# Softmax weights split into two fp16 parts and transposed by DMA, values into two scaled fp16 parts, in a two-layer attention trunk

## The chip, the core and the metric

The kernel runs on one core of a Trainium2 chip. The core has five engines that run side by side, each working through its own instructions in order: PE (TensorE, matmuls; its weight loads are listed apart as PEld), DVE (VectorE), ACT (ScalarE), POOL (GpSimd) and SP (SyncE, which here issues all DMA transfers). They meet by semaphores. PE reads SBUF and writes PSUM; 16 DMA engines move data between SBUF and the main memory, or within SBUF. The metric is the device time of one execution in microseconds.

## The reference

Two layers over a sequence of 2048 frames with 1024 features, all in float32. Each layer has a norm, one input projection, two groups of attention heads, a gate on each group, and an output projection that is added to the residual.

```python
# layer 0
z = rms_norm(x, ln_g) @ w_in
#   A: 4 heads, each with two score maps over 64 features and values 128 wide
s = q @ k.T * scale - slopes * dist;  p = softmax(masked s)
w = p[:, :, 0] - lam * p[:, :, 1]
a_out = rms_norm(w @ v, subln_g) * (1.0 - lam_init)
#   B: 8 heads, values 64 wide, frame-causal, log forget gates as bias
b_out = softmax(q @ k.T * scale + cq - cum) @ v
x = x + concat([a_out * silu(ag), b_out * silu(bg)]) @ w_out
# layer 1
#   C: 8 query heads on 2 key/value heads, window of two blocks, sinks
#   D: 8 heads, own chunk and 8 chunks before it, learned bias by distance
x = x + concat([c_out * silu(cg), d_out * silu(dg)]) @ w_out
```

All q and k are normed. In A and B a row of scores reaches back to the start of the sequence; in D it covers at most 5 blocks of 128, in C 2.

## The kernel before

The sequence is cut into 16 blocks of 128 rows (tb). The work runs unit by unit: four units of A (one head each), four of B (two heads each), the first output projection, two units of C (four query heads each), four of D (two heads each), the second output projection. Each unit has 16 steps, one per tb.

A step has four parts. `p` projects: 24 matmuls of 128x512 into the tile `z` (lines 213 to 215: input and weight are each split in a high and a low 32-bit part, and three of the four products are kept), then `evac`, `qk_prep`, and the values, split by `v_split` (or inline in A) into V (high and low part side by side, fp32r) and a bf16 copy Vb. `t` transposes q and k. `q` is `qk_row`: logits of up to 512 columns in PSUM (`pss`, line 305), added to a bias and reduced to a minimum by DVE (line 308) into `row`, then one exponential per 1024 columns on ACT (`exp_row`, line 326). `v` multiplies the weights with the values.

PE needs the weights transposed for that. `v` takes four blocks of 128x128 of `row` at a time: PE transposes them into PSUM (`ptp` at line 352, `ptA` at line 470), ACT copies the high part `pth` (fp32r, line 103) and DVE the rest `ptl` (bf16, line 107); then each block is multiplied: `pth` with V (128x128 in B, C and D, line 367; 128x256 in A, line 481), `ptl` with Vb (lines 369 and 484). In A the two score maps are first combined, row = row0 + cf * row1, on DVE (line 467) or, in odd groups of four whole blocks, on POOL (lines 464 and 465).

`drive` sets the order in which the work is written: in round i it merges projection of step i + 2, transposes of q and k of step i + 1, logits of step i, and values of step i - 1, the last from 0.4 of the round on. A scheduler then puts each engine's instructions in order. PSUM has 2 buffers for `z`, 2 for logits (pS), 3 for transposes (pT), 1 for the output of `v` (pO).

Of the kernel before, what the change touches and what calls it, by code (L numbers as in the profile page):

```python
# [25 lines left out]
SCRATCH = 1024  # L26

# [29 lines left out]
class Trunk:  # L57
    def __init__(self, ctx, tc, t):
# [8 lines left out]
        self.sm = pool("sm", 6)  # L67
        self.dram = pool("dram", 1, space=bass.MemoryType.DRAM)
# [14 lines left out]
        for i in range(2):  # L83
            g = self.const.tile([P, KB], F32, name=f"lng{i}")
            nc.sync.dma_start(g[:], t[f"ln{i}"])
            self.lng.append(g)
        self.mhalf = self.const.tile([P, 8], F32, name="mhalf")
# [84 lines left out]
    def transposed(self, xs, dst):  # L172

        nc = self.nc
        for half, x in enumerate(xs):
# [3 lines left out]
            xt = self.ap.tile([P, 4, 2, P], F32R, tag="xn", name="xnT", bufs=2)  # L179
# [15 lines left out]
    def split_x(self, st, src, dst, lo_eng):  # L195
# [3 lines left out]
        for i, (h, l, x) in enumerate(st["x"]):  # L199
            raw = self.wp.tile([P, KB // 2, P], F32, tag="xraw", name="xraw", bufs=2)  # L200
# [58 lines left out]
    def v_split(self, z):  # L259

        nc = self.nc
        V = self.kvp.tile([P, 2, P], F32R, tag="V", name="V", bufs=19)
        V4 = V[:].rearrange("p h (a d) -> p h a d", a=2)
        self.split(V4[:, :, 0], V4[:, :, 1], z.rearrange("p (h d) -> p h d", d=64), nc.scalar, nc.gpsimd)
        Vb = self.kvp.tile([P, 2, 64], BF16, tag="Vb", name="Vb", bufs=19)
        nc.scalar.activation(Vb[:].rearrange("p h d -> p (h d)"), z, AF.Copy)
        return V, Vb

    def silu2(self, z, mul=None):
# [6 lines left out]
        if mul is not None:  # L276
            nc.gpsimd.tensor_tensor(out=g[:], in0=g[:], in1=mul, op=ALU.mult)
# [43 lines left out]
    def exp_row(self, row_st, nmax):  # L321
        nc = self.nc
        s = row_st["sums"]
        rows = row_st["rows"]
        for i, (row, hm) in enumerate(rows):
            nc.scalar.activation(row[:, :hm * P], row[:, :hm * P], AF.Exp, scale=-1.0, bias=nmax, accum_out=s[:, i:i + 1])  # L326

    def two_sums(self, st):

        s = st["s"] = self.sm.tile([P, 2, 2], F32, tag="rs", name="rs")  # L330
        st["r"] = [dict(sums=s[:, h]) for h in range(2)]
# [7 lines left out]
    def heads_av(self, nh, items, r, gate, dst):  # L339
# [3 lines left out]
        groups = [items[i:i + 4] for i in range(0, len(items), 4)]  # L343
        hls = {}
        st = {}

        def tr(gi):
            g = groups[gi]
            n = len(g)
            pt = self.pT.tile([P, 4, P], F32, tag="t", name="ptp")  # L350
            for i, it in enumerate(g):
                nc.tensor.transpose(pt[:, i], it[1](), self.idf[:])  # L352
            h = ap.tile([P, 4, P], F32R, tag="pt", name="pth", bufs=5)
            l = ap.tile([P, 4, P], BF16, tag="ptl", name="ptl", bufs=5)
            hls[gi] = h, l
            self.split(h[:, :n], l[:, :n], pt[:, :n], nc.scalar, nc.vector)

        def mm(gi):
# [3 lines left out]
            h, l = hls[gi]  # L362
            g = list(enumerate(groups[gi]))
            for head in sorted({it[0] for _, it in g}):
                own = [(i, it) for i, it in g if it[0] == head]
                for i, (_, _, V, first, last) in own:
                    nc.tensor.matmul(O[:, head], h[:, i], V[0], start=first, stop=False, skip_group_check=True)  # L367
                for i, (_, _, V, first, last) in own:
                    nc.tensor.matmul(O[:, head, 0:64], l[:, i], V[1], start=False, stop=last, skip_group_check=True)  # L369

        def end():
            O = st["O"]
            o = ap.tile([P, nh, 64], F32, tag="oT", name="oT", bufs=2)
            nc.scalar.activation(o[:], O[:, :, 64:128], AF.Copy, scale=0.5)
            nc.vector.scalar_tensor_tensor(out=o[:], in0=O[:, :, 0:64], scalar=0.5, in1=o[:], op0=ALU.mult, op1=ALU.add)
# [5 lines left out]
        n = len(groups)  # L381
        for gi in range(n + 1):
            if gi < n:
                pieces.append((0.109 * len(groups[gi]), lambda gi=gi: tr(gi)))
            if gi:
                pieces.append((0.095 * len(groups[gi - 1]), lambda gi=gi: mm(gi - 1)))
# [9 lines left out]
    def unit_A(self, h, W, X):  # L396
        nc, ap = self.nc, self.ap
        slope = float(2.0 ** (-8.0 * (h + 1) / 4))
        ks, vs, steps = [], [], []

        def mk(tb):
# [3 lines left out]
            def p():  # L405
# [4 lines left out]
                pieces = self.proj(st, z, W, 512)  # L410
                if h == 0:
                    pieces.append((KB * 0.107, lambda: self.forget(st)))

                def post():
# [6 lines left out]
                    V = self.kvp.tile([P, 2, P], F32R, tag="V", name="VA", bufs=19)  # L421
                    self.split(V[:, 0, :], V[:, 1, :], z[:, 256:384], nc.scalar, nc.gpsimd)
                    Vb = self.kvp.tile([P, P], BF16, tag="Vb", name="Vb", bufs=19)
                    nc.scalar.activation(Vb[:], z[:, 256:384], AF.Copy)
                    vs.append((V, Vb))
# [12 lines left out]
            def q():  # L438
                self.two_sums(st)
                out = []  # L440

                def last():
# [3 lines left out]
                    nc.vector.reciprocal(s[:, :, 1], s[:, :, 0])  # L446
                for c in range(2):
# [3 lines left out]
            def v():  # L451
                hls = {}
                groups = [(j, min(4, m - j)) for j in range(0, m, 4)]

                def tr(gi):
                    r0, r1 = st["r"]
# [619 lines left out]
```

## Time and profile before

| | us |
|---|---|
| runs: median (lowest, highest) | 2948.31 (2943.84, 2950.85) |
| the profiled execution | 2953.78 |
| its span (first to last instruction) | 2951.9 |

The stages in the trace, from the span's start: A to about 805 us, B to 1540, the first output projection to 1800, C to 2160, D to 2760, the second output projection to the end. The projections' 512-column matmuls of layer inputs are the largest groups, over 700 us of busy time each:

```profile
L213 PE MATMUL z<-wh,x 128*128 128x512 f32 x1792 | 729.4, 408 | 16.8 <-DVE x L105 12.9
L352 PE MATMUL ptp<-idf,row 128*128 128x128 f32 x1648 | 256.5, 277 | 0.6 <-DVE ptl L107 0.6
```

A row names the line, engine, operation, the tiles written and read, the shape, the count; then the busy time and the mean of one in ns; then the idle time of the engine just before them and what ended it. Durations of matmuls overlap, so their sum is no time of PE: the distance of two starts is.

### The profile page before, as it was taken

How to read it: one execution, taken by the hardware profiler on the slowest of the kernel's cores; microseconds unless marked ns; L12 is line 12 of the kernel's file. 1: busy time of each engine (PE TensorE's matmuls, PEld its weight loads, DVE VectorE, ACT ScalarE, POOL GpSimd, SP SyncE). 2: the span in 40 equal slices, each digit the busy share in tenths (PEclk: the TensorE clock that was granted, in tenths of full speed). 3: DMA queues.
4: the chain of work that ended last, by engine and by line, in shares of the span. 5: the costliest groups of instructions: out<-in, count | busy, mean ns of one | idle time of the engine just before them, and what ended most of it. 6: DMA issues, size and time to landing. Idle time of an engine off the chain costs nothing.

```text
span 2951.9 us, 53646 instructions
## 1 busy us (share of the span) xinstructions
PE 2876.8 (97%) x18152; PEld 2435.1 (82%) x18152; DVE 1981.1 (67%) x6282; ACT 1834.3 (62%) x4821; POOL 1188.0 (40%) x1852
## 2 busy tenths in 40 slices
PE   7999999999999999999999999999999999999999
PEld 5778778787888888888888887988888888888787
DVE  6898888878877677676775335666666666666422
ACT  6567767677677666676674225777766666666310
POOL 5775565655534324432331003353334343342200
PEclk8999999999999999999999999999999999999999
DMA  8443333332333423333325644244444433342532
GB/s 299 154 133 135 127 117 117 111 125 96 112 102 105 135 86 125 122 99 121 102 67 178 215 186 159 92 135 139 144 141 141 134 132 135 120 159 93 173 129 86
DMA packets 152978, 389.43 MB, mean 132 GB/s; under 512 B 17376, under 2 KB 47072, under 8 KB 152704
## 3 DMA queue, kind: packets, MB, share of 16 engines
q1 hardware_dynamic: 152704, 385.99, 38.6%
q8 instruction: 145, 2.38, 0.3%
q14 instruction: 129, 1.06, 0.1%
HBM read 318.75 MB, written 67.17 MB: 131 GB/s over the span
## 4 chain that ended last, share of the span: by engine, by line
PE 74%; DVE 11%; POOL 5%; ACT 4%; issue 3%; DMA 3%; SPq 0%; POOLq 0%; DVEq 0%; ACTq 0%
PE z L213 11%; PE z L214 11%; PE z L215 11%; PE pss L305 8%; PE ptp L352 7%; PE OT L367 6%; PE zo L213 4%; PE zo L215 4%; PE zo L214 4%; DVE row L308 3%; PE OT L369 2%; PE ptq L247 2%; POOL y L115 1%; DVE ptl L107 1%; DVE row L467 1%
## 5 line engine op out<-in xcount | busy, mean ns | idle before, releaser
L213 PE MATMUL z<-wh,x 128*128 128x512 f32 x1792 | 729.4, 408 | 16.8 <-DVE x L105 12.9
L215 PE MATMUL z<-wh,x 128*128 128x512 f32 x1792 | 717.3, 401 | 4.4 <-POOL x L107 3.6
L214 PE MATMUL z<-wl,x 128*128 128x512 f32 x1792 | 718.2, 401 | 2.7 <-POOL wl L107 1.7
L326 ACT ACTIVATE row<-row,mx 128x1024 f32<-128x1024 f32 (+7 forms) x512 | 440.2, 861 | 186.4 <-DVE mx L308 181.1
L305 PE MATMUL pss<-kT,qT 128*128 128x512 f32 (+3 forms) x1728 | 501.3, 373 | 20.3 <-DVE mx L308 18.5
L213 PEld LDWEIGHTS z<-wh,x 128*128 128x128 f32 x1792 | 342.0, 191 | 76.4 <-ACT wh L152 10.3
L215 PEld LDWEIGHTS z<-wh,x 128*128 128x128 f32 x1792 | 341.2, 190 | 71.1 <-POOL x L107 5.7
L214 PEld LDWEIGHTS z<-wl,x 128*128 128x128 f32 x1792 | 342.0, 191 | 61.5 <-DVE wl L153 4.3
L107 DVE TENSOR_TENSOR ptl<-ptp,pth 128x512 bf16<-128x512 f32 (+1 forms) x518 | 326.2, 640 | 77.1 <-ACT pth L103 74.6
L103 ACT ACTIVATE pth<-ptp 128x512 fp32r<-128x512 f32 (+1 forms) x518 | 276.0, 556 | 123.0 <-PE ptp L352 120.0
L305 PEld LDWEIGHTS pss<-kT,qT 128*128 128x128 f32 x1728 | 292.5, 190 | 62.3 <-DVE mx L308 27.7
L367 PE MATMUL OT<-V,pth 128*128 128x128 f32 x1896 | 314.0, 278 | 0.1
L115 POOL TENSOR_TENSOR y<-v,mhalf 128x4 f32<-128x4 f32 (+2 forms) x326 | 292.2, 898 | 19.4
L367 PEld LDWEIGHTS OT<-V,pth 128*128 128x128 f32 x1896 | 281.9, 193 | 14.6 <-ACT pth L103 0.6
L352 PE MATMUL ptp<-idf,row 128*128 128x128 f32 x1648 | 256.5, 277 | 0.6 <-DVE ptl L107 0.6
L107 POOL TENSOR_TENSOR hl<-zs,hl 128x256 fp32r<-128x256 f32 (+1 forms) x240 | 175.1, 730 | 187.9 <-DVE hl L105 144.2
L221 ACT ACTIVATE zs<-z,rs 128x512 f32<-128x512 f32 (+1 forms) x240 | 160.3, 669 | 118.3 <-PE z L215 110.3
L352 PEld LDWEIGHTS ptp<-idf,row 128*128 128x128 f32 x1648 | 191.2, 142 | 22.5 <-PE pss L305 1.0
L107 POOL TENSOR_TENSOR V<-zs,V 128x128 fp32r<-128x128 f32 x144 | 67.2, 468 | 334.8 <-ACT V L103 331.2
L369 PE MATMUL OT<-Vb,ptl 128*128 128x64 bf16 x1896 | 177.2, 198 | 1.5 <-DVE ptl L107 1.5
L107 POOL TENSOR_TENSOR wl<-wraw,wh 128x512 fp32r<-128x512 f32 x118 | 154.1, 1310 | 46.0 <-ACT wh L103 43.6
L117 DVE TENSOR_TENSOR q<-y 128x4 f32<-128x4 f32 (+2 forms) x326 | 85.6, 263 | 126.5 <-POOL y L115 124.8
(180 smaller groups left out, 5785.8 us busy)
## 6 DMA issues: line engine op xcount, KB each, us to landing
x<-xs SPq DMA_DIRECT2D x416, 512.0 KB, 3.6
wraw<-in_w_dram SPq DMA_DIRECT2D x64, 256.0 KB, 2.8
xs<-x SPq DMA_DIRECT2D x32, 512.0 KB, 4.1
xs<-xnT SPq DMA_DIRECT2D x32, 512.0 KB, 5.2
xraw<-in_xT_dram SPq DMA_DIRECT2D x32, 256.0 KB, 3.9
x<-in_x_dram SPq DMA_DIRECT2D x32, 256.0 KB, 6.0
mixa<-out SPq DMA_DIRECT2D x128, 64.0 KB, 2.0
biasB<-cumd SPq DMA_DIRECT2D x32, 256.0 KB, 4.3
```

The source lines that it names most:

```text
L103: nc.scalar.activation(hi, src, AF.Copy)
L107: lo_eng.tensor_tensor(out=lo, in0=src, in1=h, op=ALU.subtract)
L115: nc.gpsimd.tensor_tensor(out=y[:], in0=v[:], in1=self.mhalf[:, :n], op=ALU.pow)
L213: nc.tensor.matmul(ps(), xh[:, i, :], wh, start=(kb == 0), stop=False)
L214: nc.tensor.matmul(ps(), xh[:, i, :], wl, start=False, stop=False)
L215: nc.tensor.matmul(ps(), xl[:, i, :], wh, start=False, stop=(kb == KB - 1))
L221: self.nc.scalar.activation(zs[:, :n], z[:, :n], AF.Copy, scale=self.rs[layer][:, tb:tb + 1])
L305: nc.tensor.matmul(ps[:, :w], q()[:, j, :], k[:, slot, (b % 4) * P:(b % 4) * P + w], start=(j == 0), stop=(j == 1))
L326: nc.scalar.activation(row[:, :hm * P], row[:, :hm * P], AF.Exp, scale=-1.0, bias=nmax, accum_out=s[:, i:i + 1])
L352: nc.tensor.transpose(pt[:, i], it[1](), self.idf[:])
L367: nc.tensor.matmul(O[:, head], h[:, i], V[0], start=first, stop=False, skip_group_check=True)
L369: nc.tensor.matmul(O[:, head, 0:64], l[:, i], V[1], start=False, stop=last, skip_group_check=True)
```

## The change

The weights are no longer transposed by PE. As soon as a row's exponential is there, `weights_T` splits it where it lies, by rows: ACT writes the high part as fp16, scaled by 2^15 (in A by a factor per row), DVE the low part as fp16 behind it in the same tile `ph`, and one DMA on SP's queue transposes both from SBUF to SBUF into `pT`. `v` then only multiplies, with both operands in fp16. The order of the work in `v` loses the pieces for transposes, and the work of `weights_T` is issued in `q`.

Values become two fp16 parts, V, without Vb. So that they fit fp16, each column of values is scaled by a power of two taken from the sum of squares of its weights' column: `v_scale` computes it once per unit (8 squares on POOL, 8 matmuls with ones, a few integer steps on DVE). DVE multiplies the values by `inv`; the inverse `sc` goes into the gate on POOL (B, C, D) or onto A's output on DVE. In A the coefficients of the combination are worked out in `q`, with four more single-column steps, and every odd group of blocks goes to POOL. The logits get a third PSUM buffer, the transposes lose one; `xraw` and `xnT` share the buffers of `ph` and `pT`.

```diff
-        self.pS = pool("pS", 2, space=bass.MemoryType.PSUM)
-        self.pT = pool("pT", 3, space=bass.MemoryType.PSUM)
+        self.pS = pool("pS", 3, space=bass.MemoryType.PSUM)
+        self.pT = pool("pT", 2, space=bass.MemoryType.PSUM)
...
+    def v_scale(self, W, c, bias):
...
+        def square(kb):
...
+            w = W[kb][0][:, c:c + P].bitcast(F32)
+            nc.gpsimd.tensor_tensor(out=sq[0][:, kb], in0=w, in1=w, op=ALU.mult)
+        def sums():
+            ps = self.pT.tile([P, P], F32, tag="t", name="psw")
+            for kb in range(KB):
+                nc.tensor.matmul(ps[:], self.ones[:], sq[0][:, kb], start=(kb == 0), stop=(kb == KB - 1))
...
+    def v_split(self, z, inv, heads):
+        nc = self.nc
+        nc.vector.tensor_tensor(out=z, in0=z, in1=inv[:], op=ALU.mult)
+        V = self.kvp.tile([P, heads, 2, P // heads], F16, tag="V", name="V", bufs=19)
+        self.split(V[:, :, 0], V[:, :, 1], z.rearrange("p (h d) -> p h d", h=heads), nc.scalar, nc.gpsimd)
+        return V
+
+    def weights_T(self, w, n, scale=PSC):
+        nc, ap = self.nc, self.ap
+        hl = ap.tile([P, 2048], F16, tag="ph", name="ph", bufs=3)
+        nc.scalar.activation(hl[:, :n], w, AF.Copy, scale=scale)
+        nc.vector.scalar_tensor_tensor(out=hl[:, n:2 * n], in0=w, scalar=scale, in1=hl[:, :n], op0=ALU.mult, op1=ALU.subtract)
+        pt = ap.tile([P, 16, P], F16, tag="pt", name="pT", bufs=PTB)
+        nc.sync.dma_start_transpose(out=pt[:, :2 * n // P], in_=hl[:, :2 * n])
+        return pt[:, :2 * n // P].rearrange("p (a b) q -> p a b q", a=2)
...
             nc.scalar.activation(row[:, :hm * P], row[:, :hm * P], AF.Exp, scale=-1.0, bias=nmax, accum_out=s[:, i:i + 1])
+            if row_st.get("T") is not None:
+                row_st["T"].append(self.weights_T(row[:, :hm * P], hm * P))
...
-        def tr(gi):
...
-                nc.tensor.transpose(pt[:, i], it[1](), self.idf[:])
...
-            self.split(h[:, :n], l[:, :n], pt[:, :n], nc.scalar, nc.vector)
...
+            for head, w, V, first, last in own:
+                nc.tensor.matmul(O[:, head], w()[:, 0], V().rearrange("p a d -> p (a d)"), start=first, stop=False, skip_group_check=True)
+            for head, w, V, first, last in own:
+                nc.tensor.matmul(O[:, head, 0:64], w()[:, 1], V()[:, 0], start=False, stop=last, skip_group_check=True)
...
+                    cf = self.sm.tile([P, 4], F32, tag="cf", name="cf")
+                    st["r0"], kap = cf[:, 3:4], cf[:, 2:3]
+                    nc.vector.tensor_scalar(out=cf[:, 0:1], in0=s[:, 1, 1:2], scalar1=s[:, 0, 0:1], scalar2=self.nlam[:, 0:1], op0=ALU.mult, op1=ALU.mult)
+                    nc.vector.scalar_tensor_tensor(out=cf[:, 1:2], in0=cf[:, 0:1], scalar=-1.0, in1=cf[:, 0:1], op0=ALU.mult, op1=ALU.max)
+                    nc.vector.tensor_scalar(out=cf[:, 1:2], in0=cf[:, 1:2], scalar1=1.0 / PSC, scalar2=1.0 / PSC, op0=ALU.mult, op1=ALU.add)
+                    nc.vector.reciprocal(kap, cf[:, 1:2])
+                    nc.vector.tensor_tensor(out=st["r0"], in0=cf[:, 1:2], in1=s[:, 0, 1:2], op=ALU.mult)
...
+                            if i % 2:
+                                nc.gpsimd.tensor_scalar(out=t1, in0=t1, scalar1=cf[:, 0:1], scalar2=1.0, op0=ALU.mult, op1=ALU.mult)
+                                nc.gpsimd.tensor_tensor(out=t0, in0=t1, in1=t0, op=ALU.add)
+                            else:
+                                nc.vector.scalar_tensor_tensor(out=t0, in0=t1, scalar=cf[:, 0:1], in1=t0, op0=ALU.mult, op1=ALU.add)
+                        st["T"].append(self.weights_T(w0[:, :n * P], n * P, kap))
...
+                    nc.vector.tensor_tensor(out=o[:], in0=o[:], in1=u["sc"][:], op=ALU.mult)
```

Three places show what stands in a row. Line numbers of the changed kernel are its own: 218 to 220 are the projection (213 to 215 before), 347 the logits (305), 394 and 396 the high and low product (367 and 369), 485 the combination (467), 198 the load of x (193).

PE in B, block tb = 9 of a unit, before: the weights' transposes stand among the projection's matmuls, and the products close behind them.

```order
L305 MATMUL pss_18872<-kT_18247,qT_18661 128x384 x2
L352 MATMUL ptp_18920<-idf_87,row_18710 128x128 x2
L213 MATMUL z_19048<-wh_15272,x_18641 128x512
L214 MATMUL z_19048<-wl_15273,x_18641 128x512
L215 MATMUL z_19048<-wh_15272,x_18641 128x512
L352 MATMUL ptp_18944<-idf_87,row_18710 128x128 x4
L367 MATMUL OT_18911<-V_16924,pth_18889 128x128
L367 MATMUL OT_18911<-V_17187,pth_18889 128x128
```

The same place now: the products read `pT`, which a DMA wrote; the last logits of that row (`pss_17490`) stand 54 projection matmuls ahead of the first product.

```order
L218 MATMUL z_18135<-wh_13760,x_17756 128x512
L219 MATMUL z_18135<-wl_13761,x_17756 128x512
L220 MATMUL z_18135<-wh_13760,x_17756 128x512
L394 LDWEIGHTS pT_17517
L394 MATMUL OT_17632<-V_15884,pT_17517 128x128
```

No transpose of weights is left on PE, and each product brings its own weight load of a 16-bit block.

SP, the queue of DMAs, in B around the outputs of tb = 8 and 9 (`mixa8`, `mixa9`), before: loads of x, of weights, and the outputs.

```order
L379 DMA mixa8_145<-out_18833 128x128
L193 DMA x_19044<-xs0_15_120 128x1024
L193 DMA x_19256<-xs0_0_105 128x1024
L379 DMA mixa9_146<-out_19040 128x128
L193 DMA x_19257<-xs0_0_105 128x1024
L150 DMA wraw_17963<-in_w0_dram 128x512
```

Now each row of scores adds a transposing DMA per 1024 columns (16 blocks: 8 high, 8 low; 6 blocks: 3 and 3).

```order
L406 DMA mixa8_150<-out_17571 128x128
L307 DMA_TRANSPOSE pT_17621<-ph_17618 128x16x128
L307 DMA_TRANSPOSE pT_17627<-ph_17624 128x6x128
L155 DMA wraw_16796<-in_w0_dram 128x512
L198 DMA x_17937<-xs0_0_110 128x1024
L155 DMA wraw_16937<-in_w0_dram 128x512
L198 DMA x_17938<-xs0_0_110 128x1024
L307 DMA_TRANSPOSE pT_17692<-ph_17689 128x16x128
L155 DMA wraw_17087<-in_w0_dram 128x512
L307 DMA_TRANSPOSE pT_17698<-ph_17695 128x6x128
L406 DMA mixa9_151<-out_17753 128x128
```

The loads of x and of weights stand in the same queue, between the transposes. There are 448 transposing DMAs in all: 150 of 16 blocks, 120 of 10, the rest of 2 to 14; 4880 blocks together.

DVE in A, where the two score maps of a block are combined, before: the sums' reciprocal, the coefficient, then the combinations with `cf`, and between them the logits of the next block.

```order
L446 RECIPROCAL rs_5481<-rs_5481 128x2
L493 SCALAR_TENSOR_TENSOR out_5857<-OA_5723,rs_5295,out_5857 128x128
L460 TENSOR_SCALAR cf_5920<-rs_5481,nlam_325 128x1
L308 ISA row_5877,mx_5876<-pss_5896,distA_192,mx_5876 128x512
L308 ISA mx_5876 128x1
L467 SCALAR_TENSOR_TENSOR row_5682<-row_5746,cf_5920,row_5682 128x512
L467 SCALAR_TENSOR_TENSOR row_5707<-row_5779,cf_5920,row_5707 128x512
L467 SCALAR_TENSOR_TENSOR row_5707<-row_5779,cf_5920,row_5707 128x384
```

Now (a block of the same length):

```order
L469 RECIPROCAL rs_5173<-rs_5173 128x2
L110 CAST hl_5501<-zs_5477 128x4x64
L242 TENSOR_TENSOR zs_5684<-zs_5684,y_5693 128x256
L472 TENSOR_SCALAR cf_5452<-rs_5173,nlam_330 128x1
L473 SCALAR_TENSOR_TENSOR cf_5452<-cf_5452 128x1
L485 SCALAR_TENSOR_TENSOR row_5356<-row_5405,cf_5452,row_5356 128x512
L485 SCALAR_TENSOR_TENSOR row_5381<-row_5431,cf_5452,row_5381 128x512
L474 TENSOR_SCALAR cf_5452<-cf_5452 128x1
L110 CAST hl_5709<-zs_5684 128x4x64
L475 RECIPROCAL cf_5452<-cf_5452 128x1
L476 TENSOR_TENSOR cf_5452<-cf_5452,rs_5173 128x1
```

Four single-column steps are new, and the group of 384 columns has gone to POOL; the split of 1024 columns out of `row` follows a few rows later on DVE.

More of the change, by code (lines that the diff above doesn't have):

```diff
@@ L26 @@
 SCRATCH = 1024
+PTB = 6
+PSC = 2.0 ** 15
 class Step:
@@ L276, in silu2 @@
         if mul is not None:
-            nc.gpsimd.tensor_tensor(out=g[:], in0=g[:], in1=mul, op=ALU.mult)
+            o = g[:] if len(mul.shape) == 2 else g[:].rearrange("p (h d) -> p h d", h=mul.shape[1])
+            nc.gpsimd.tensor_tensor(out=o, in0=o, in1=mul, op=ALU.mult)
         return g
@@ L326, in exp_row, with two_sums @@
             nc.scalar.activation(row[:, :hm * P], row[:, :hm * P], AF.Exp, scale=-1.0, bias=nmax, accum_out=s[:, i:i + 1])
-    def two_sums(self, st):
+            if row_st.get("T") is not None:
+                row_st["T"].append(self.weights_T(row[:, :hm * P], hm * P))
+    def two_sums(self, st, own=True):
         s = st["s"] = self.sm.tile([P, 2, 2], F32, tag="rs", name="rs")
-        st["r"] = [dict(sums=s[:, h]) for h in range(2)]
+        st["r"] = [dict(sums=s[:, h], T=[] if own else None) for h in range(2)]
     def add_sums(self, st):
@@ L342, in heads_av, with mm @@
         nc, ap = self.nc, self.ap
-        groups = [items[i:i + 4] for i in range(0, len(items), 4)]
-        hls = {}
         st = {}
-        def tr(gi):
[L348 to L355, printed above, removed]
-            self.split(h[:, :n], l[:, :n], pt[:, :n], nc.scalar, nc.vector)
-        def mm(gi):
+        def mm(own):
             if "O" not in st:
@@ L380, in heads_av @@
         pieces = []
[L381 to L386, printed above, removed]
+        for head in range(nh):
+            own = [it for it in items if it[0] == head]
+            pieces += [(0.09 * len(own[i:i + 4]), lambda g=own[i:i + 4]: mm(g)) for i in range(0, len(own), 4)]
         pieces.append((0.0, end))
@@ L398, in unit_A @@
         slope = float(2.0 ** (-8.0 * (h + 1) / 4))
-        ks, vs, steps = [], [], []
+        ks, vs, u = [], [], {}
         def mk(tb):
@@ L451, in v @@
             def v():
[L452 to L456, printed above, removed]
-                    j, cm = groups[gi]
-                    if gi == 0:
-                        cf = st["cf"] = self.sm.tile([P, 1], F32, tag="cf", name="cf")
-                        nc.vector.tensor_scalar(out=cf[:], in0=st["s"][:, 1, 1:2], scalar1=st["s"][:, 0, 0:1], scalar2=self.nlam[:, 0:1], op0=ALU.mult, op1=ALU.mult)
-                        st["O"] = self.pO.tile([P, 2, P], F32, tag="o", name="OA")
-                    t0, t1 = (r["rows"][j // 8][0][:, j % 8 * P:(j % 8 + cm) * P] for r in (r0, r1))
-                    if gi % 2 and cm == 4:
-                        nc.gpsimd.tensor_scalar(out=t1, in0=t1, scalar1=st["cf"][:, 0:1], scalar2=1.0, op0=ALU.mult, op1=ALU.mult)
-                        nc.gpsimd.tensor_tensor(out=t0, in0=t1, in1=t0, op=ALU.add)
-                    else:
-                        nc.vector.scalar_tensor_tensor(out=t0, in0=t1, scalar=st["cf"][:, 0:1], in1=t0, op0=ALU.mult, op1=ALU.add)
-                    pt = self.pT.tile([P, 4, P], F32, tag="t", name="ptA")
-                    for i in range(cm):
-                        nc.tensor.transpose(pt[:, i], t0[:, i * P:i * P + P], self.idf[:])
-                    h = ap.tile([P, 4, P], F32R, tag="pt", name="pth", bufs=5)
-                    l = ap.tile([P, 4, P], BF16, tag="ptl", name="ptl", bufs=5)
-                    hls[gi] = h, l
-                    self.split(h[:, :cm], l[:, :cm], pt[:, :cm], nc.scalar, nc.vector)
```

112 lines of the change are left out of this document (59 added, 53 removed).

## The prediction, made before the changed kernel ran

> **What bounds the kernel now.** I read the page's busy shares first, then the table of stretches (cut at the stages: units A, units B, first output projection, C, D, second output projection), then PE's waits, then the chain that ended last.
>
> ```profile
> span 2951.9 us, 53646 instructions
> PE 2876.8 (97%) x18152; PEld 2435.1 (82%) x18152; DVE 1981.1 (67%) x6282; ACT 1834.3 (62%) x4821; POOL 1188.0 (40%) x1852
> core 0: us, PE busy (x) PEld busy (x) DVE busy (x) ACT busy (x) POOL busy (x), PEclk, DMA share, GB/s
> 0.00:805.00 805.00, 756.90 (x4390) 614.36 (x4391) 667.63 (x2046) 546.99 (x1472) 503.99 (x752) 0.98 0.41 139
> 805.00:1540.00 735.00, 728.54 (x5228) 628.45 (x5228) 530.56 (x1732) 508.93 (x1250) 279.06 (x468) 1.00 0.33 107
> 1800.00:2160.00 360.00, 356.04 (x2362) 314.80 (x2361) 235.25 (x836) 260.17 (x774) 142.93 (x219) 0.99 0.39 129
> 2160.00:2760.00 600.00, 592.11 (x3841) 509.86 (x3840) 385.67 (x1323) 398.25 (x1075) 235.04 (x362) 0.99 0.39 131
> PE pss L305 <- DVE mx L308: 18.5, 28, 1.9
> PE 74%; DVE 11%; POOL 5%; ACT 4%; issue 3%; DMA 3%; SPq 0%; POOLq 0%; DVEq 0%; ACTq 0%
> ```
>
> PE is busy in 97% of the span, its granted clock is 0.98 to 1.00, its longest wait sums to 18.5 us. So PE's own instructions set the time, and what leaves PE shortens the kernel, up to the point where another engine is full. The nearest is DVE: 668 of 805 us (83%) in A, 531 of 735 (72%) in B, 386 of 600 (64%) in D. In A it is closer than the mean says:
>
> ```profile
> 240.00:430.00 190.00, 184.00 (x1093) 150.71 (x1091) 166.42 (x500) 131.69 (x350) 117.88 (x177) 1.00 0.38 126
> ```
>
> Here DVE works 166 of 190 us (88%) while PE is still the bound with 97%.
>
> **What PE loses.** A matmul's duration overlaps the next one's, so its price is the distance of starts in the timeline of PE (columns: start, us, instruction, count).
>
> ```profile
> 1022.39 0.39 PE L213 MATMUL z<-wh,x 128*128 128x512 f32 x1
> 1022.62 0.39 PE L214 MATMUL z<-wl,x 128*128 128x512 f32 x1
> 1022.85 0.60 PE L352 MATMUL ptp<-idf,row 128*128 128x128 f32 x4
> 1023.20 0.48 PE L215 MATMUL z<-wh,x 128*128 128x512 f32 x1
> 1023.52 0.60 PE L352 MATMUL ptp<-idf,row 128*128 128x128 f32 x4
> ...
> 999.85 0.50 PE L367 MATMUL OT<-V,pth 128*128 128x128 f32 x3
> 1000.19 0.45 PE L215 MATMUL z<-wh,x 128*128 128x512 f32 x1
> 1000.48 0.29 PE L369 MATMUL OT<-Vb,ptl 128*128 128x64 bf16 x4
> 1000.61 0.64 PE L367 MATMUL OT<-V,pth 128*128 128x128 f32 x4
> ...
> 303.03 0.40 PE L484 MATMUL OA<-Vb,ptl 128*128 128x128 bf16 x4
> 303.24 0.36 PE L481 MATMUL OA<-VA,pth 128*128 128x256 f32 x1
> ```
>
> Four transposes take 1023.20 - 1022.85 = 0.35 us, and the projection matmul behind them 0.32 instead of 0.23, its weights being loaded late. So a transpose costs (0.35 + 0.09)/4 = 0.11 us. There are 2440: 544 in A (60 us), 1088 in B (120), 248 in C (27), 560 in D (62), in all 269 us. The high product of weights and values (L367) takes 0.34/3 = 0.113 us with both operands in 32 bits. The same shape in 16 bits is L484: 0.21/4 = 0.053. Its 1896 instances save 0.06 each: 65 us in B, 15 in C, 34 in D. The low product is 16-bit already (0.13/4 = 0.033) and stays; A's high product is 256 wide and is taken as unchanged. The sums of squares add 104 matmuls of 128x128 at 0.053, 6 us. With PE alone in charge the stages would be A 805 - 60 + 2 = 747, B 735 - 185 + 2 = 552, C 319, D 506, and the span 2576.
>
> **What DVE, ACT and POOL get.** The split moves from behind the transpose to ahead of it, with as many elements: ACT writes the high part, DVE the low part, now out of SBUF and up to 1024 wide.
>
> ```profile
> L107 DVE TENSOR_TENSOR ptl<-ptp,pth 128x512 bf16<-128x512 f32 x430 | 290.5, 685 | 72.0 <-ACT pth L103 70.3
> L107 DVE TENSOR_TENSOR ptl<-ptA,pth 128x512 bf16<-128x512 f32 x112 | 75.8, 683 | 4.4 <-ACT pth L103 4.2
> L467 DVE SCALAR_TENSOR_TENSOR row<-row,cf 128x512 f32<-128x512 f32 x72 | 62.9, 893 | 0.4
> L467 DVE SCALAR_TENSOR_TENSOR row<-row,cf x120: 336/752/1781, 36.4 to 794.2; 128x512 f32<-128x512 f32 x72, 128x128 f32<-128x128 f32 x16, 128x256 f32<-128x256 f32 x16, 128x384 f32<-128x384 f32 x16
> L376 DVE TENSOR_TENSOR oT<-oT,rs 128x128 f32<-128x128 f32 x128 | 47.7, 373 | 1.3
> L460 DVE TENSOR_SCALAR cf<-rs,nlam 128x1 f32<-128x1 f32 x64 | 17.2, 269 | 0.8
> L446 DVE RECIPROCAL rs<-rs 128x2 f32<-128x2 f32 x64 | 10.3, 161 | 9.9 <-ACT row L326 9.1
> ```
>
> The new low part is bounded by 0.685 us per 512 elements (old split) and 0.893 (L467, the same operation out of SBUF); I take the middle, 0.79, since no reason excludes either. A: old split out, -93 (136 groups of 512 at 0.683); new split, +107; 24 of 120 row combinations go to POOL, -18 (0.752 each); values times scale and output times scale, 2 x 64 x 0.373 = +48; four new single-column steps per block, 256 at 0.16 to 0.27, +55; powers of two, +7 (six small steps per unit, about 0.3 each). Sum +106: 668 becomes 774, more than the 747 that PE needs. B: new split against old, 272 groups x 0.1 = +28, values times scale +24, powers +7: 531 becomes 590, more than PE's 552. D: +14 +24 +7 makes 431, under PE's 506.
>
> DVE won't work without waits. It waits for PE and ACT now, in the stretch above 12% of the time, though PE set the pace there. I take 94%, with 88% and 100% as ends: **A 774/0.94 = 823 (774 to 880), B 590/0.94 = 628 (590 to 670).** So what is late next after the transposes are gone is DVE, and A gains nothing. In D PE stays the bound: 506 at today's PE share of 98.7% is 513. C: 319 + 5 = 324. ACT loses the copies Vb, and its 547 of 805 us in A leave room; POOL's new gate products (128 of 128x128) and squares go into the 456 us that it has free in B and the 300 in A. The moved buffers cost nothing as I see it: xraw and xnT share tiles with ph and pT, but xraw is loaded in A's first unit alone and xnT is written in the output projection, where few rows are split; the PSUM pool that gives a buffer to the logits lost its most frequent users, the transposed weights.
>
> **What the DMA queue gets.** 4880 blocks of 128x128 in 16 bits, 32 KB each, 160 MB in 448 transfers, nowhere shown in this trace. The nearest rows:
>
> ```profile
> x<-xs SPq DMA_DIRECT2D x416, 512.0 KB, 3.6
> mixa<-out SPq DMA_DIRECT2D x128, 64.0 KB, 2.0
> ```
>
> From 64 to 512 KB the landing grows by 1.6 us for 14 blocks: 0.114 us per block if a transposing transfer runs like a copy. If each block took its share of the small transfer's 2.0 us with no overlap, it would be 1.0. I take a value near the first, since the large copy shows that transfers overlap within themselves, and keep 1.0 as the far end. At 0.114, B's 2176 blocks take 248 of 628 us and hide behind DVE and PE; DMA share in B is 0.33 now.
>
> The wait that is added is PE's wait for pT. Behind it all of PE queues. In the new order of PE, 54 projection matmuls (12.3 us at 0.228) besides logits and other products stand between the last logits of the row shown in the diff's place in B and its first use. The chain in that time is exponential, high part, low part, transfer:
>
> ```profile
> L326 ACT ACTIVATE row<-row,mx 128x1024 f32<-128x1024 f32 x160 | 183.6, 1148 | 94.5 <-DVE mx L308 90.7 <-POOL y L115 2.6
> ```
>
> 1.15 + 1.15 + 1.6 + 3.6 = 7.5 us. So I price the wait at nothing; uncovered it would be a few us in each of the 64 blocks of a kind.
>
> [...]
>
> **Sum.** 2951.9 + 18 (A) - 107 (B) - 36 (C) - 87 (D) = 2740 of span, 2742 beside the profiled 2953.8. The runs' median, 2948.3, is 5 lower: **2735 us**. With the ends of A and B: 2650 to 2840.
>
> **Rivals.**
> 1. *The transfers set the pace in B; slower than before.* SP is one queue. B may take 840 us, which is 735 plus all that A, C and D give (105), before the kernel is slower: 840/2176, so the point that decides is 0.39 us per block. At 0.45 us B takes 979, D 504 (still hidden), the kernel 2952 + 18 + 244 - 36 - 87 = 3091 of span, **3085**. For it: 0.39 lies between my bounds, and small packets land slowly (32 GB/s in the 64 KB row). Against it: the 512 KB row, and DMA two thirds idle.
> 2. *DVE keeps up.* If the low part costs 0.685 per 512 and DVE runs without waits, PE stays the bound: 2576 of span, **2580** with a little waiting. For it: the three logits tiles in place of two let DVE run ahead. Against it: today's 12% of waits in A.
> 3. *The transfers cost something but not all:* 0.3 to 0.38 us per block, B 653 to 827, **2760 to 2935**; the change is then hidden partly. That the transposes stay on PE is excluded: no row of the new order has them.
>
> **How the numbers follow.** Forecast (2650 to 2840) 0.52; rival 2 down to 2580, 0.12; upper part of rival 3, 0.08; within 0.2% (about what a measurement of this kernel can tell from no change), 0.04; rival 1, 0.24. Faster 0.72, same 0.04, slower 0.24. The range 2600 to 3085 leaves out half of rival 2 and half of rival 1.
>
> **What would show it.** Right: no ptp or ptA on PE; OT with 128 columns at starts 0.053 apart; DVE over 90% busy in A, whose length is 800 to 850; B about 630; pT landing in under 6 us. Wrong: PE idle with pT as releaser, PE's share in B under 80%, a median landing of pT that grows with its size by more than 0.39 us per block (rival 1); DVE under 85% with A under 770 (rival 2). The prediction falls if DVE's instructions get slower beside the transfers, or if A's rows reach pT later than PE asks for them.

## The result, and the profile after

| | before | after |
|---|---|---|
| median of the runs (lowest, highest), us | 2949.58 (2943.84, 2953.53) | 2813.93 (2808.18, 2817.92) |
| span of the profiled execution, us | 2951.9 | 2806.1 |

The ratio is 0.954, with a 95% interval of 0.9517 to 0.9563: 4.6% faster, where 7.3% was predicted. The head of the changed kernel's page; then its view of the DMA (the queue: packets, MB, share of 16 engines; the issues: count, KB each, median us to landing); then the queue's row of the kernel before:

```profile
span 2806.1 us, 50570 instructions
PE 2577.2 (92%) x15816; PEld 2085.1 (74%) x15816; DVE 2119.1 (76%) x6635; ACT 1787.5 (64%) x4383; POOL 1449.2 (52%) x2164
```

```profile
q1 hardware_dynamic: 791680, 545.96, 76.5%
x<-xs SPq DMA_DIRECT2D x416, 512.0 KB, 4.4
pT<-ph SPq DMA_TRANSPOSE x448, 4.5
```

```profile
q1 hardware_dynamic: 152704, 385.99, 38.6%
```

PE fell from 97% to 92% busy, and the kernel is not bound by PE everywhere any more. The queue carries 160 MB more (4880 blocks of 32 KB), in 639,000 packets more, and its engines' share has doubled. To see where, the stages are cut in both traces by the same marks: A ends with the last product of OA, B, C and D with their last logits on DVE, and C begins with its first. (The prediction's cuts lay elsewhere, B's end 31 us earlier and C's start 12, so B is 763 here and 735 there. What is compared with its forecast is therefore differences: by these cuts it expects 763 - 107 = 656 of B.)

| us | A | B | first output projection | C | D | rest |
|---|---|---|---|---|---|---|
| before | 808.4 | 763.0 | 240.6 | 341.6 | 606.1 | 192.2 |
| after | 840.2 | 692.9 | 240.3 | 317.6 | 527.9 | 187.2 |
| difference | +32 | -70 | 0 | -24 | -78 | -5 |
| predicted | +18 | -107 | 0 | -36 | -87 | 0 |

The table of stretches (A without its first 60 us, B, C, D), with the same columns as in the prediction, before:

```profile
60.00:808.40 748.40, 719.01 (x4249) 586.73 (x4250) 634.26 (x1934) 505.34 (x1354) 474.74 (x698) 0.99 0.37 124
808.40:1571.40 763.00, 756.54 (x5456) 652.66 (x5454) 551.36 (x1788) 529.04 (x1289) 280.81 (x469) 1.00 0.32 105
1812.00:2153.60 341.60, 337.64 (x2258) 298.82 (x2258) 225.23 (x798) 249.20 (x741) 132.04 (x200) 0.99 0.38 129
2153.60:2759.70 606.10, 598.21 (x3874) 515.05 (x3873) 389.36 (x1338) 404.56 (x1098) 238.47 (x368) 0.99 0.39 131
```

And after:

```profile
60.00:840.20 780.20, 689.54 (x3748) 533.34 (x3747) 708.79 (x2266) 507.43 (x1253) 550.62 (x788) 0.95 0.62 163
840.20:1533.10 692.90, 620.81 (x4431) 501.66 (x4428) 573.91 (x1759) 503.24 (x1125) 364.45 (x549) 0.95 0.97 215
1773.40:2091.00 317.60, 303.29 (x2034) 259.87 (x2034) 241.94 (x802) 244.21 (x700) 175.84 (x245) 0.98 0.74 188
2091.00:2618.90 527.90, 506.78 (x3368) 418.51 (x3367) 413.07 (x1373) 389.98 (x994) 287.13 (x447) 0.99 0.91 218
```

Each stage has another limit. In D and C PE is busy 96% and 95%. In A DVE leads with 91% (PE 88%). In B no engine is full, PE 90% and DVE 83%, but the last but one column says 0.97: the 16 DMA engines are. The waits of the whole span (us in total, times, longest us) show who feels it:

```profile
ACT ph L304 <- DMA pT<-ph: 83.4, 59, 6.3
PEld L394 <- DMA pT<-ph: 75.1, 63, 6.6
PE OT L394 <- DMA pT<-ph: 55.9, 48, 6.1
PE pss L347 <- DVE mx L350: 49.4, 53, 3.5
PE OA L497 <- DMA pT<-ph: 28.4, 24, 3.0
```

PE waits for the transposed weights in A (L497) and, of the waits of L394, mostly in B; the view of B alone has

```profile
PE OT L394 <- DMA pT<-ph: 39.4, 32, 6.1
```

The first row of the list is the other end of the same queue: ACT can't write the next high part, because a transfer still reads the tile ph.

**The price of a block.** The queue's share gives it: (0.765 x 2806.1 - 0.386 x 2951.9)/4880 = 0.206 us of all 16 engines per block, where the prediction took 0.114. In B the loads of before need 0.32 x 763 = 244 us of the engines, the 2176 blocks 449, together 693. B lasts 693.

### The profile page after: what moved, and what is told of

Its sections match the earlier page's. It is cut to its first block, busy times and chain, and to the rows that moved or that the text cites. A ratio compares the mean times of both kernels' runs of the same rounds, so it can differ in the third digit from the quotient of the medians.

```text
span 2806.1 us, 50570 instructions
## 1 busy us (share of the span) xinstructions
PE 2577.2 (92%) x15816; PEld 2085.1 (74%) x15816; DVE 2119.1 (76%) x6635; ACT 1787.5 (64%) x4383; POOL 1449.2 (52%) x2164
## 5 line engine op out<-in xcount | busy, mean ns | idle before, releaser
L347 PE MATMUL pss<-kT,qT 128*128 128x512 f32 (+3 forms) x1728 | 482.4, 378 | 60.2 <-DVE mx L350 49.4
L347 PEld LDWEIGHTS pss<-kT,qT 128*128 128x128 f32 x1728 | 300.0, 195 | 131.8 <-DVE mx L350 68.4
L305 DVE SCALAR_TENSOR_TENSOR ph<-row,ph 128x1024 f16<-128x1024 f32 (+6 forms) x320 | 294.3, 925 | 66.9 <-ACT ph L304 64.8
L304 ACT ACTIVATE ph<-row 128x1024 f16<-128x1024 f32 (+6 forms) x320 | 236.6, 746 | 84.8 <-DMA pT<-ph 81.9
L112 POOL TENSOR_TENSOR hl<-zs,hl 128x256 fp32r<-128x256 f32 (+1 forms) x240 | 194.3, 810 | 132.1 <-DVE hl L110 90.6
L394 PE MATMUL OT<-V,pT 128*128 128x128 f16 x1896 | 200.1, 226 | 61.6 <-DMA pT<-ph 55.9
L394 PEld LDWEIGHTS <-pT 128*128 128x128 f16 x1896 | 121.4, 101 | 120.6 <-DMA pT<-ph 75.1
L112 POOL TENSOR_TENSOR V<-zs,V 128x128 f16<-128x128 f32 x208 | 107.0, 518 | 115.8 <-ACT V L108 108.1
L245 POOL TENSOR_TENSOR zs<-zs,g 128x128 f32<-128x128 f32 x144 | 79.9, 555 | 150.5 <-DVE zs L242 129.4
L108 ACT ACTIVATE x<-psm 128x512 fp32r<-128x512 f32 x64 | 38.1, 596 | 187.1 <-PE zo L220 141.2
L118 POOL TENSOR_SCALAR v<-ssq 128x4 f32<-128x4 f32 (+1 forms) x240 | 55.6, 232 | 195.2 <-DVE ssq L236 160.5
```

What stands on the lines that cost most here:

```text
L112: lo_eng.tensor_tensor(out=lo, in0=src, in1=h, op=ALU.subtract)
L304: nc.scalar.activation(hl[:, :n], w, AF.Copy, scale=scale)
L305: nc.vector.scalar_tensor_tensor(out=hl[:, n:2 * n], in0=w, scalar=scale, in1=hl[:, :n], op0=ALU.mult, op1=ALU.subtract)
L347: nc.tensor.matmul(ps[:, :w], q()[:, j, :], k[:, slot, (b % 4) * P:(b % 4) * P + w], start=(j == 0), stop=(j == 1))
L394: nc.tensor.matmul(O[:, head], w()[:, 0], V().rearrange("p a d -> p (a d)"), start=first, stop=False, skip_group_check=True)
```

## The experiments

Each run was timed beside the kernel before, whose median was 2949.5 to 2953.8 there. "End of B" is the length of A and B together, which doesn't depend on where the cut between them falls: 1571.4 before, 1533.1 after.

### The fp16 products alone

The kernel before, with both parts of weights and values in fp16 and no scales; the transposes stay on PE, and the PSUM pools are those of before.

```diff
-        V = self.kvp.tile([P, 2, P], F32R, tag="V", name="V", bufs=19)
+        V = self.kvp.tile([P, 2, P], F16, tag="V", name="V", bufs=19)
...
-            h = ap.tile([P, 4, P], F32R, tag="pt", name="pth", bufs=5)
-            l = ap.tile([P, 4, P], BF16, tag="ptl", name="ptl", bufs=5)
+            h = ap.tile([P, 4, P], F16, tag="pt", name="pth", bufs=5)
+            l = ap.tile([P, 4, P], F16, tag="ptl", name="ptl", bufs=5)
```

> The kernel before, with PE's transposes kept, and only the types of the products changed: pth, ptl, V and Vb are fp16, no scaling. Prediction's term (0.06 us less per high product with 128 columns, 1896 of them, in a kernel whose bound is PE): 114 us faster than before, about 2835. Rival (the distance of the high products is set by what stands between them and not by their type): within 30 us of 2949.

Measured: 2836.95 us (2834.89 to 2838.15), ratio 0.9613 (0.9599 to 0.9628). That is 114 us less than the 2951.23 of the kernel before, timed beside it. A 802, B 711, C 320, D 573. So the smaller half of the diff brings most of the gain, and all the rest of it (269 us of transposes off PE, the scales, the third logits buffer) brings only the 23 us from there to the changed kernel: A +38, B -18, C -2, D -45.

### The low part: without its transfer, then without its computation

```diff
-        nc.sync.dma_start_transpose(out=pt[:, :2 * n // P], in_=hl[:, :2 * n])
-        return pt[:, :2 * n // P].rearrange("p (a b) q -> p a b q", a=2)
+        nc.sync.dma_start_transpose(out=pt[:, :n // P], in_=hl[:, :n])
+        return pt[:, None, :n // P].broadcast_to([P, 2, n // P, P])
```

In the second run the instruction L305 goes too. PE does as many products as after the change, since the high part stands in for the low.

> The changed kernel, but only the high part is transposed (the low product multiplies the high part once more; the low part is still computed). Half the transposed blocks, 2440 in place of 4880; all else is as in the changed kernel. Theory 1 (in B the DMA engines are the bound: busy 97% there, 0.206 us of all 16 engines per block): B, 693 us in the changed kernel from A's last product to B's last logits, falls to 620-640, A (840 to its last product) and D (528) stay within 10, the whole about 2750. Theory 2 (DVE is the bound in B too, as the prediction had it): B stays within 10 of 693, the whole within 15 of 2814.

> As the run with the high part alone, and DVE's operation for the low part is left out too (about 100 us of DVE time in A, 130 in B). Theory 1 alone: like the run before it within 15 us. Theory 2 (DVE bound): A falls from 840 to about 770, B to about 600, the whole 2640 to 2690. If A falls and B does not, DVE binds A and the transfers B.

Measured: 2741.49 us (ratio 0.9293, 0.9278 to 0.9309) with half the transfers, 2655.74 (0.9000, 0.8987 to 0.9014) with DVE's low part gone too. The stretches of A and B of the first, then of the second:

```profile
60.00:827.20 767.20, 689.87 (x3758) 537.88 (x3757) 717.20 (x2260) 507.79 (x1255) 560.56 (x786) 0.95 0.51 144
827.20:1467.80 640.60, 599.21 (x4445) 485.40 (x4442) 571.81 (x1767) 500.59 (x1131) 382.80 (x550) 0.98 0.77 179
```

```profile
60.00:785.80 725.80, 670.01 (x3755) 528.96 (x3754) 633.55 (x2168) 505.06 (x1255) 516.66 (x786) 0.98 0.55 152
785.80:1391.40 605.60, 587.48 (x4440) 478.83 (x4438) 412.97 (x1578) 500.44 (x1126) 313.97 (x550) 1.00 0.80 189
```

B falls by 52 us when the DMA share falls from 0.97 to 0.77, with DVE as busy as before (572 us): the first theory, and DVE's work is not what held B at 693. Without the low part it falls by 35 more, and then PE is 97% busy at a clock of 1.00; this is the range of the second theory. So limits lie close together in B: the transfers at 693, at 641 something that goes with the low part (DVE's work, or its place in the chain ahead of the transfer; the run doesn't tell which), PE at 606. D stays (527.9, 530.5, 525.0): PE. A moves little when transfers go (-13), and by 41 more when DVE's low part goes.

### Every transfer twice

```diff
         nc.sync.dma_start_transpose(out=pt[:, :2 * n // P], in_=hl[:, :2 * n])
+        nc.sync.dma_start_transpose(out=pt[:, :2 * n // P], in_=hl[:, :2 * n])
```

> Every transposing transfer is issued twice, into the same tile; nothing is left out. Theory, the DMA engines' time is the price (0.206 us of all 16 per block, from the first runs) and it adds to the loads: stage B 244 + 2 x 449 = 1142 us, D 249 + 2 x 231 = 711, C about 340, A 840 to 860 because its engines have room (484 + 224 of 780); span about 3470. Rival, issuing on SP is the price (about 1.2 to 1.9 us per transfer, SP busy 577 of 693 us in B): 192 more issues make B 577 + 192 x 1.6 = 880 and leave D under 600; span about 3030. Second rival, DVE sets B: no change, 2806.

Measured: 3468.1 us (3462.63 to 3470.23), ratio 1.1755 (1.1726 to 1.1784), slower than the kernel before. The stretches of A, B and D, then its view of the DMA:

```profile
60.00:882.20 822.20, 701.37 (x3757) 541.05 (x3756) 717.22 (x2276) 512.31 (x1258) 551.14 (x791) 0.94 0.84 199
882.20:1943.80 1061.60, 761.38 (x4401) 581.59 (x4398) 566.12 (x1750) 510.12 (x1115) 348.10 (x543) 0.78 0.99 204
2565.70:3270.40 704.70, 578.63 (x3344) 457.17 (x3343) 404.25 (x1366) 386.82 (x984) 285.98 (x448) 0.89 0.96 217
```

```profile
q1 hardware_dynamic: 1430656, 705.92, 88.0%
pT<-ph SPq DMA_TRANSPOSE x896, 4.4
```

B grows by 369 us to 1062 at a DMA share of 0.99, 80 less than the 1142 expected, D by 177 to 705 (711 expected), and A by 42, more than expected, though its DMA engines are busy 0.84 of the time. The rival of the issues, at 1.6 us each, gave B only 880. It is not quite out of the game: the issues in B took 2.2 us on average, not 1.6, and SP was busy 942 us of B's 1062 (577 of 693 in the changed kernel). But that is 89% and 83%, where the DMA engines have 0.99 and 0.97. The second copies cost (0.880 x 3460.9 - 0.765 x 2806.1)/4880 = 0.184 us each, a tenth less than the first ones. With half the transfers the same sum gives (0.630 x 2734.4 - 0.386 x 2951.9)/2440 = 0.24; the share in that sum is from its page:

```profile
q1 hardware_dynamic: 479360, 466.00, 63.0%
```

So the price is 0.18 to 0.24 us, by three counts, and it adds to the loads. These counts charge the blocks with what the loads lose beside them: the packets of 4096 bytes took 862 us of 16 engines before the change and 903 after it. The trace also has every packet: those of 256 bytes, 128 to a block, took 0.196 us of 16 engines per block after the change, 0.210 with half the transfers and 0.185 with all of them twice. DVE's 566 us in B didn't change, and B grew all the same, so the second rival is out.

### Long rows of B half on PE

In B the second tile of long rows (blocks from 8 on) is transposed on PE and split from PSUM; all else as after the change.

```diff
-            if row_st.get("T") is not None:
+            if row_st.get("T") is not None and not (i and row_st.get("pe")):
...
+                    for i in range(n):
+                        o = (4 * g - 8 + i) * P
+                        nc.tensor.transpose(pt[:, i], row[:, o:o + P], self.idf[:])
...
+                    nc.scalar.activation(hi, pt[:, :n], AF.Copy, scale=PSC)
+                    nc.vector.scalar_tensor_tensor(out=lo, in0=pt[:, :n], scalar=PSC, in1=hi, op0=ALU.mult, op1=ALU.subtract)
```

> The changed kernel, but in B the second exponential of a row (blocks 8 and up, 288 of B's 1088) is transposed by PE in 32 bits and split out of PSUM into the same two fp16 parts. DMA engines lose 576 blocks x 0.206 = 119 us in B, PE gets 288 x 0.11 = 32 us. Theory 1: B falls from 693 to about 640, the whole to about 2760, faster than both kernels. Theory 2: no gain, 2815 to 2850.

Measured: 2806.08 us (2803.75 to 2811.19), ratio 0.9512 (0.9498 to 0.9526). That lies between the two theories. B takes 674.5, not 640, and D, in which nothing was edited, takes 12 us more (why is open), so against the changed kernel's 2813.93 the gain is hardly more than the scatter. The DMA share in B fell to 0.86, so that the engines no longer were its limit; at the same time PE got its transposes back. What holds B at 674 was not shown.

### A back on PE

Unit A with PE's transposes, two fp16 parts and values without scale, B, C and D as after the change; once with the changed kernel's PSUM pools (3 buffers for logits, 2 for transposes) and once with those of before (2 and 3).

```diff
-                        st["T"].append(self.weights_T(w0[:, :n * P], n * P, kap))
...
+                    for i in range(cm):
+                        nc.tensor.transpose(pt[:, i], t0[:, i * P:i * P + P], self.idf[:])
+                    h = hls[gi] = ap.tile([P, 2, 4, P], F16, tag="pt", name="pth", bufs=PTB)
+                    self.split(h[:, 0, :cm], h[:, 1, :cm], pt[:, :cm], nc.scalar, nc.vector)
```

> Unit A back on PE's transposes with two fp16 parts of weights and values (as in the run of the fp16 products alone), values not scaled there; B, C and D as after the change. Theory, what A lost lies in A's own DVE work and chain: A 802, B 693, C 318, D 528, span 2768, median 2774: faster than both. Rival, A lost because the PSUM pools are 3 and 2 instead of 2 and 3 buffers: A stays at 830 to 850 and the median at 2800 to 2820.

> As the mix before, but the PSUM pools of the logits and of the transposes have 2 and 3 buffers, as before the change. Theory: A 802 as in the run of the fp16 products, B held by the DMA engines at 693, so the same 2774 within 10. Rival, the third logits buffer is what lets DVE run ahead in B, C and D: those lose 10 to 40 us together and the median is 2785 to 2815.

Measured: 2769.2 us (ratio 0.9387, 0.9367 to 0.9407) and 2818.08 (0.9553, 0.953 to 0.9575). A takes 790 and 793 in them, 51 and 47 less than after the change, so what A lost is not in the pools. B takes 701 and 725, D 530 and 548: the pools of 3 and 2 are worth some 40 us in B and D, which the prediction had named as something for DVE but priced at nothing.

This bears on what the transposing transfers themselves are worth. With the pools of before, B and D of the run with the fp16 products alone, then of this mix:

```profile
801.90:1512.60 710.70, 702.67 (x5435) 573.65 (x5432) 537.20 (x1785) 521.65 (x1286) 278.83 (x469) 1.00 0.36 112
2075.80:2648.90 573.10, 566.73 (x3909) 473.97 (x3908) 384.88 (x1330) 402.31 (x1091) 234.53 (x364) 0.99 0.43 139
```

```profile
792.80:1517.80 725.00, 631.55 (x4434) 497.08 (x4431) 571.86 (x1773) 513.56 (x1139) 355.54 (x553) 0.96 0.94 205
2080.70:2628.30 547.60, 515.93 (x3297) 419.56 (x3298) 419.32 (x1363) 392.40 (x987) 293.44 (x443) 0.97 0.89 209
```

At equal pools the transfers (with the scales) cost 14 us in B and 5 in C (325 against 320) and gain 25 in D. Most of the rest that B, C and D gained over the fp16 products came with the third logits buffer. Whether the kernel with PE's transposes would gain as much from that buffer was not run; A, with its transposes on PE, lost nothing by having two buffers for them.

A of the mix, then PE's longest wait in it:

```profile
60.00:789.60 729.60, 703.97 (x4247) 552.10 (x4246) 639.04 (x1936) 490.61 (x1292) 471.24 (x705) 1.00 0.40 127
```

```profile
PE pss L347 <- DVE mx L350: 10.9, 13, 2.7
```

PE sets A again (96%, clock 1.00), though it has the 544 transposes to do. The same wait in A of the changed kernel, beside that for pT:

```profile
PE pss L347 <- DVE mx L350: 34.8, 36, 3.5
PE OA L497 <- DMA pT<-ph: 28.4, 24, 3.0
```

### What holds A

Two theories for A: DVE's work, or the chain combine, high part, low part, transfer. Three runs. First, the values aren't scaled (L295 left out). Second, A's products are ordered a step later:

```diff
+        def vs(i):
+            return [j for j in (i - 2, i - 1) if (j < 4 * NT) == (j == i - 2)]
...
-                   (*wq, marked(timed(get(i, "q"), *wq, at, w))), (*wv, marked(timed(get(i - 1, "v"), *wv, at, w)))])
+                   (*wq, marked(timed(get(i, "q"), *wq, at, w))), *((*wv, marked(timed(get(j, "v"), *wv, at, w))) for j, wv in zip(vs(i), ((0, .5) if len(vs(i)) > 1 else (0, .85) if i < 4 * NT + 1 else wv, wv)))])
```

Third, both.

> Left out: the multiplication of the values with their power of two on DVE (208 instructions of 0.36 us, 23 us in each of A, B and D, 6 in C); the factors at the end are still applied, so the output is off by them. Theory, DVE sets A alone, and the DMA engines B, PE C and D: A 840 - 23/0.9 = 814, all others unchanged; median about 2788. Rival, A waits for the chain high part, low part, transfer and not for DVE's work: no change, 2808 to 2815. Second rival, DVE is late in B too: B 693 - 25 = 668, median about 2763.

> Nothing left out; in unit A the products of weights and values of a row are ordered one step later, so that the chain combine, high part, low part, transfer has a step of PE's work more before its result is asked for. Theory, A is held by this chain: the waits of PE for pT (41 + 28 us in A) nearly go and A comes to 770 to 800; B, C and D as after the change; median 2740 to 2775. Rival, A is held by DVE's work (709 of 780 us busy): A 830 to 840, median 2800 to 2815. Second rival, the waits move from pT to the logits' buffers (pss waits for DVE): A 810 to 830, median 2780 to 2805.

> Both at once: A's products of weights and values one step later, and the multiplication of the values with their power of two left out (the factors at the end are still applied, so the output is off by them). Each alone left A at 839 to 844 us. Theory, A has two limits close together, DVE's work and the chain to pT, and moves only when both are eased: A 839 - 23/0.93 = 814, median 2799 - 25 = 2774. Rival, neither is the limit (A is held by the DVE to GpSimd to DVE steps of the norm, 16 to 31 us of DVE's waiting, or by PE's clock of 0.95): A 830 to 845, median 2790 to 2805.

Measured: 2810.14 us without the scale (ratio 0.9521, 0.9496 to 0.9545), 2798.68 one step later (0.9485, 0.9469 to 0.9501), 2805.74 with both (0.9513, 0.9491 to 0.9535). A ends at 843.7, 839.1 and 827.9, B at 1541.6, 1513.9 and 1522.2. Without the scale DVE had 208 instructions less in all and A was no shorter, as the chain's theory had it. One step later A was no shorter either, as DVE's theory had it, and with both edits A fell by 12 us, not by 26, and the whole kernel by hardly more than the scatter. A's end is its last product, which the second edit itself moves; but the start of A's last logits on DVE, which it doesn't move, says the same: 814.5 us after the change, 812.7 a step later, 800.7 with both. So neither holds A alone, and the two together are not the whole of it. The norm's steps between DVE and POOL, named as a rival in the last of these expectations, were not tested. A step later PE still waited for pT, about as long as after the change; its stretch of A and that wait:

```profile
60.00:839.10 779.10, 689.14 (x3774) 531.65 (x3773) 725.22 (x2273) 509.93 (x1262) 551.50 (x788) 0.96 0.65 164
```

```profile
PE OA L497 <- DMA pT<-ph: 28.1, 22, 3.6
```

B ended 19 us earlier there, and the whole kernel was 15 us faster; A gained only 2 of these by its last logits, and with both edits B's end lay only 11 earlier. Where they come from is open. The timeline of the changed kernel in A shows how the two theories hang together (columns: start, us, instruction, and in brackets how long the engine had waited and for whom):

```profile
727.23 1.04 PE L497 MATMUL OA<-V,pT 128*128 128x256 f16 x4 [2.52 <-DMA pT<-ph]
729.73 0.91 PE L347 MATMUL pss<-kT,qT 128*128 128x512 f32 x2
730.85 0.37 ACT L508 ACTIVATE out<-OA,cf 128x128 f32<-128x128 f32 x1 [3.06 <-PE OA L500]
731.25 0.35 DVE L509 SCALAR_TENSOR_TENSOR out<-OA,cf,out 128x128 f32<-128x128 f32 x1 [1.99 <-ACT out L508]
731.52 0.74 DVE L350 CUSTOM_DVE_ANT_0 row<-pss,distA,mx 128x512 f32<-128x512 f32 x1
```

PE waits 2.5 us for a transfer, the logits of L347 stand behind it in PE's order, ACT waits for the product, DVE waits 2.0 us for ACT, and the next row's logits queue behind DVE's L509. One late transfer stops three engines in turn, and two of them, PE and DVE, are 88 and 91% busy in A and have little time to make up for it. It is a reading of one place; no run singled out the loop, so which of its links would have to go is open.

### The parts put together

A one step later with B half on PE; and A back on PE with B half on PE.

> As the run with A's products one step later, and in B the second tile of long rows (blocks from 8 on) transposed on PE, as in the hybrid run. Theory: the two gains add, since they lie in different stages: A 770 to 800, B 675 as in the hybrid, median 2725 to 2765. Rival: B starts later against its own loads and gains nothing, median as that of the run with A later alone.

> Unit A back on PE's transposes with fp16 parts, B's long rows half on PE, C and D as after the change. Theory: A 790 as in the mix, B 675 as in the hybrid, median 2740 to 2755. Rival: the hybrid's 18 us in B came from what A left it, B stays at 700, median 2765 to 2775.

Measured: 2806.52 us (ratio 0.9514, 0.9496 to 0.9532) and 2751.13 (0.9332, 0.9317 to 0.9348). The first is a miss: B ends at 1512.5, as with the half of B on PE alone (1512.1). The second is the fastest kernel of the study that leaves nothing out, 198 us under the kernel before (2949.54 beside it) and 63 under the changed one; like the mix it has no scale on A's values. Its A and B:

```profile
60.00:792.60 732.60, 707.60 (x4252) 554.50 (x4250) 639.13 (x1938) 491.05 (x1294) 471.91 (x706) 0.99 0.39 126
792.60:1464.40 671.80, 631.34 (x4641) 509.30 (x4638) 569.07 (x1793) 504.25 (x1163) 352.49 (x551) 0.97 0.85 194
```

PE is 97% busy in A, and in B PE (94%), DVE (85%) and the DMA engines (0.85) share the load. So the choice by stages is A's transposes on PE, those of C, D and the first half of long rows in B by DMA. What is shown of it is A (51 us better on PE) and D (25 us better by DMA at equal pools); half of B was compared only with all of B by DMA.

## Why the prediction came out as it did

The sign and the kind were right: the time falls, and PE stops being the only bound. The gain was 66 us too large (-212 forecast for the span, -146 measured), and all four stages came out above their forecast. The time still lies in the range, near its upper end, because the range was wide; it was made wide for DVE's waits, not for the transfers that filled it in B. To that extent it is luck. Of the signs that the text gave, A's length (840), DVE's share there (91%) and the landing of pT (4.5 us) came as for right; B's length did not, and PE idle with pT as releaser came as for wrong. By its own steps:

- **PE loses the high products' 114 us: right.** The run with these alone gave 114. Their price after the change is (1003.59 - 1003.36)/4 = 0.058 us each by the starts below, 0.053 predicted.

```profile
1003.36 0.40 PE L394 MATMUL OT<-V,pT 128*128 128x128 f16 x4
1003.59 0.28 PE L396 MATMUL OT<-V,pT 128*128 128x64 f16 x4
```

- **PE loses the transposes' 269 us, and DVE is late next in A and B at 94% busy: the first half right, the second not shown in A and wrong in B.** They left PE, but behind them stood other limits at once. DVE is the busiest engine in A, but A was no shorter without the 23 us of the scale; without the low part it was 41 shorter, and that is work of DVE and a link of the chain at once.
- **B, 628 predicted: the step that failed is "At 0.114, B's 2176 blocks take 248 of 628 us and hide behind DVE and PE".** It is a term of the wrong size, 0.206 us in place of 0.114, and a sum not made: the loads already took 243 us of the same engines, so hiding ended at (628 - 243)/2176 = 0.177 us per block (0.189 by the cuts above: 656 and 244). The text set the price only against 0.39, the point at which the whole kernel would be slower. This is the mechanism of the third rival, at a smaller price than the 0.3 to 0.38 it named, with loads and transposes added up instead of the transposes alone. By the copy's price the engines would have been busy 243 + 248 = 491 us and hidden. The run with half the transfers has that load (0.77 x 641 = 493), and there B was 122 us shorter than before, more than the 107 forecast: DVE's work in B had grown by 20 us and not by 59.
- **The low part at 0.79 us per 512: too dear.** It took 0.66 in its long form, less than both bounds (here rival 2 was right; its DVE without waits did not come), and DVE's busy time in A came to 746 us, not 774 (its group of long rows, then the stretch of all of A):

```profile
L305 DVE SCALAR_TENSOR_TENSOR ph<-row,ph 128x1024 f16<-128x1024 f32 x80 | 105.5, 1321 | 11.6 <-ACT ph L304 11.3
```

```profile
0.00:840.20 840.20, 731.73 (x3904) 564.07 (x3905) 746.44 (x2399) 545.34 (x1355) 583.45 (x851) 0.95 0.64 175
```

- **A, 823 predicted, +18: measured +32.** Two errors partly cancel, DVE's work 28 us too large and its share of time 89% instead of 94%. "I price the wait at nothing" failed here: PE waits 28 us for pT in A, and moving the products a step later didn't remove it. That DVE's work alone would set A, as the step had it, fell with the run without the scale. What was shown is that A is 51 us shorter with its transposes on PE and 54 shorter with neither low part nor its transfer; which link of the way by DMA costs them is open.
- **C and D, -36 and -87: measured -24 and -78.** PE bounds both, as said (95% and 96% busy); PE has a few waits that the 98.7% taken from before left out.
- **Rival 1, transfers set the pace in B:** they do, but at half the price that would have made the kernel slower. Doubling them made it so: 3468 us.
- **A transposing transfer priced like a copy, 0.114 us per block: not so.** Here 32 KB in 0.206 us of all engines is 159 GB/s. By the packets in the traces, those of 4096 bytes took 187 ns each on average before the change, so 32 KB, eight of them, took 0.094 us of 16 engines; the 128 packets of 256 bytes of a transposed block took 24.5 ns each after it, 0.196 us.

## What to carry to other kernels

Price a transfer that is to hide by adding it to what the same DMA engines already do in that stage, and compare the sum with the time that the stage would have afterwards, not with the time it has today. Before moving work off a full engine, look at the engine that is next: in the prediction's stretch of A, DVE was 88% busy while PE set the pace, and A got longer with less work on PE. A change of several parts is worth running by parts: here the narrower data type alone gave 114 us and all the rest together 23, and the choice stage by stage beat both kernels. A detail of the diff can outweigh its main part: the third logits buffer was worth some 40 us in B and D, where the transfers with their scales gained 6 in B, C and D at equal pools.

## What the runs showed of the hardware

- The transposing transfers between SBUF tiles moved in small packets: 639,000 packets more for 4880 blocks, 131 per block, or 250 bytes each on average; 0.206 us of 16 engines, or 3.3 us of one, over 131 packets is 25 ns each. A plain 512 KB load landed in 3.6 us before and 4.4 beside them.
- In B the granted clock was lower where PE waited more: 1.00 before (PE 99% busy), 0.95 after (90%), 0.78 with doubled transfers (72%). The instructions themselves took longer there: 4431 of B took PE 620.8 us at 0.95, and 4440 took 587.5 at 1.00 in the run without the low part. The share of busy time alone doesn't give the clock: it was 0.94 at 89% in the mix and 0.96 at 87% in the mix with the pools of before.
- DVE, reading an fp32 row and its fp16 high part from SBUF, needed 1.32 us for 1024 columns (0.66 per 512), where the split's subtraction out of PSUM took 0.685 per 512.
